# A decoder trunk with an RWKV recurrence: its small products chained in phases between dense work, and four row groups in the second channel mixer

## The chip, the cores and the metric

The kernel runs on one core of one Trainium2 chip. The metric is the device time of one execution in microseconds, as the median of several runs. A profiled execution stands beside them; its trace gives each instruction's start, duration and what it waited for.

The engines are named as in the profile: PE (TensorE, matrix products; PEld is its weight load), DVE (VectorE), ACT (ScalarE), POOL (GpSimd) and SP (SyncE, which issues the transfers).

## What is computed

The reference is one inference step of a two-layer trunk for 512 prompt tokens (one sequence) and 32 sample tokens (8 sequences of 4), with 1024 features. Every layer is a channel mixer, a token mixer and a second channel mixer, each with a normalisation ahead of it:

```python
def swiglu(x, wg, wu, wd):
    return (jax.nn.silu(x @ wg) * (x @ wu)) @ wd

for i in range(DEPTH):                                   # DEPTH = 2
    x = x + 0.5 * swiglu(rmsnorm(x, norm_ffa[i]), ffa_wg[i], ffa_wu[i], ffa_wd[i])   # D_FF = 2816
    x = x + mixer[i % 2](rmsnorm(x, norm_mix[i]))        # 0: RWKV-7, 1: mLSTM
    x = x + 0.5 * swiglu(rmsnorm(x, norm_ffb[i]), ffb_wg[i], ffb_wu[i], ffb_wd[i])
y = rmsnorm(x, norm_final)
```

The change is in layer 0, whose token mixer is a recurrence over 16 heads with a state of 64 x 64 per head. The samples start from a given state and the prompt from zero:

```python
def step(S, inp):
    r_t, d_t, k_t, v_t, kk_t, b_t = inp
    sa = jnp.einsum('bhvk,bhk->bhv', S, -kk_t)
    S = S * d_t[:, :, None, :] + sa[..., None] * b_t[:, :, None, :] + v_t[..., None] * k_t[:, :, None, :]
    return S, jnp.einsum('bhvk,bhk->bhv', S, r_t)
```

After it come a normalisation over each head, a bonus term (r k r_k) v, a gate g and the output projection wo. All states are returned too.

## The kernel before

Activations lie feature-major: eight tiles of 128 features x 544 tokens. The tokens are worked in two parts, `PARTS` = 0:256 and 256:544, the second with the samples at its end. Dense work is fp32 in two halves: `split` rounds a value to its high part (ACT, L352) and takes the difference as the low part (DVE, L353), and `mm3` makes three products of a 128 x 128 weight tile and 256 or 288 columns (L356 to L358). `weight` loads a weight block (SP), up to 1024 columns, and splits it in blocks of 512.

**The recurrence** (`rwkv`) works in chunks of 64 tokens. Two neighbouring tiles of 128 features, so four heads, go together: this is a group `m`. There are ND = 4 of them in each token part, so eight in all, of four chunks `c` each; `rwkv_slots` goes through 32 slots t = 4 m + c. What a group needs:

- `rwkv_prep`: low-rank products, decays and scaled rows (mostly DVE and ACT);
- `rwkv_quad`: masked products (L937), then the inverse of each chunk's triangular tile by doubling, five levels of two products with an ACT copy and DVE additions between them, in half precision, then one correction. Its products are 64 x 64 (name `b`); its transposes are products too (L945 for the rows `xt`);
- `rwkv_tokens`: values by token, `uv`, and the bonus;
- `rwkv_chunk`, per slot: a chain on one state: `pr` (L1059, L1061 into `pc`), a DVE copy, `pu` (L1042), two copies into `uv`, the state's product `pn` (L1048) and the output `py` (L1035, L1037), then the new state on DVE;
- `rwkv_sample`, second part only, once per feature tile: the samples' masked products, a state solve of three steps, outputs (L1127) and the new state (L1135), with POOL, ACT and DVE between;
- `rwkv_finish`, once per feature tile: centring (L1151), variance (L1155), the gate's product (L356 to L358 and L1168, into `ps`), each waiting for the one ahead of it through ACT and DVE.

**The dense work around it** are units in a list `todo`: first the projections of the second token part and the channel mixer that stands ahead of the recurrence, then (scope `rw2`) the output projection and the second channel mixer's first part, `ffn_units(*after, 0)`. That mixer goes in groups of hidden rows, `groups=(0, 8, 15, FT)` with FT = 22 tiles: the `up` units of a group (gate and up products), then eight `down` units over the group's rows, each added into x (L502). Every slot issues the group's small work and then its share of the units (`step`), counted in units.

**What sets the order.** The program's order in which the code issues work isn't the engines' order. A scheduler places the instructions of every engine when the kernel is built, from modelled times, and prefers what has high priority: small work is issued under `high_priority(OFF)`, so it goes in as soon as the model finds it ready, among the dense products. On the chip each engine then runs its list strictly in that order and waits where an operand isn't there.

Of the kernel before, what the change touches and what calls it, by code (L numbers as in the profile page):

```python
# [28 lines left out]
OFF = 20000  # L29
NMX = 19  # L30
# [218 lines left out]

class Trunk:  # L250
    def __init__(self, tc, nc, a, o, pool):
        self.tc, self.nc, self.a, self.o, self.pool = tc, nc, a, o, pool
        self.n = 0
        self.last = None
        self.hn = {}
        self.V, self.S, self.G, self.T = nc.vector, nc.scalar, nc.gpsimd, nc.tensor

# [97 lines left out]
    def mm3(self, out, wh, wl, xh, xl, start, stop):  # L355
        self.T.matmul(out, wh, xh, start=start, stop=False)  # L356
        self.T.matmul(out, wh, xl, start=False, stop=False)  # L357
        self.T.matmul(out, wl, xh, start=False, stop=stop)  # L358
# [102 lines left out]
    def ffn_units(self, name, g, i, groups=(0, 8, 15, FT)):  # L461
# [18 lines left out]
        def up(m):  # L480
            pg, pu = self.bank("pd", 2), self.bank("pd", 2)
            for ps, n in ((pg, "_g"), (pu, "_u")):
                wt = self.weight(self.a[name + n][m])
                for k in range(KT):
                    c = slice(k * P, (k + 1) * P)
                    self.mm3(ps[:, :w_], *wt(c), xs[k][0], xs[k][1], k == 0, k == KT - 1)
            s, w, e = self.t1(w_), self.t1(w_), self.t1(w_)
            V.tensor_tensor(s, pg[:, :w_], rs, op=ALU.mult)  # L488
            V.tensor_tensor(w, pu[:, :w_], rs, op=ALU.mult)
            self.sigmoid(e, s)  # L490
            G.tensor_tensor(s, s, w, op=ALU.mult)
            G.tensor_tensor(s, s, e, op=ALU.mult)
            h[m] = [self.hm(w_) for _ in range(2)]
            self.split(*h[m], s)

        def down(m, k0, k1):
            wt = self.weight(self.a[name + "_d"][m][:, k0 * P:k1 * P])
            ps = self.bank("pd", 2)
            for k in range(k0, k1):
                c = slice((k - k0) * P, (k - k0 + 1) * P)  # L500
                self.mm3(ps[:, :w_], *wt(c), h[k][0], h[k][1], k == k0, k == k1 - 1)
# [55 lines left out]
    def rwkv(self, before=None, after=None):  # L557


        with self.scope("rw", nps=1):  # L560
# [4 lines left out]
            with self.tc.tile_pool(name="spill", bufs=1, space=DRAM) as dp:  # L565
# [3 lines left out]
                self.d, self.quad, self.st = {}, {}, {}  # L569
                self.chain, self.chain_y = [self.bank("pc", 2) for _ in range(2)]  # L570
                self.nhm = {"mx": NMX, "hm": 8}
                with self.scope("rw1", nps=0):
# [7 lines left out]
                    with self.tc.high_priority(OFF):  # L580
                        self.rwkv_ahead(0)
                        self.rwkv_square(0)
# [3 lines left out]
                    with self.tc.high_priority(OFF):  # L586
                        self.rwkv_value(0)
                        self.rwkv_ahead(1)
# [4 lines left out]
                    self.rwkv_slots(10, 16)  # L593
                self.nhm = {"hm": 16}
                with self.scope("rw2", nps=0):
                    with self.tc.high_priority(OFF):
                        self.rwkv_value(ND)
                    self.rwkv_slots(16, 17)
# [100 lines left out]
    def part_dense(self, w, ps, xs, mw=P, first=True, last=True):  # L699
        for k in range(KT):  # L700
            c = slice(k * mw, (k + 1) * mw)
            self.mm3(ps, *w(c), xs[k][0], xs[k][1], first and k == 0, last and k == KT - 1)

    def rwkv_project(self, n, c, i):
# [12 lines left out]
        return [lambda: xs.extend(self.rwkv_mix(c, i))] + [lambda m=m: unit(m) for m in range(KT)]  # L717

    def rwkv_low_rank(self, i):
# [36 lines left out]
        for c, ns in ((1, (("r_w1", P, slice(0, 64), self.hwa),)), (4, (("r_a1", P, slice(64, P), self.hwa),)),  # L756
                      (5, (("r_g1a", P, slice(0, P), self.hg), ("r_g1b", P, slice(0, 96), None)))):
            us.append(lambda c=c: mix(c))
# [3 lines left out]
    def rwkv_first(self, i):  # L762

        low, k = self.rwkv_low_rank(i), self.rwkv_project("k", 2, i)
        return ([lambda: self.rwkv_norm(i)] + low[:4] + self.rwkv_project("r", 0, i) + k[:5],
# [26 lines left out]
    def rwkv_ahead(self, m):  # L792

        if m < 2 * ND:
            self.d[m] = [self.rwkv_prep(2 * (m % ND) + a, m // ND) for a in range(2)]

    def rwkv_square(self, m):
        if m < 2 * ND:
            self.quad[m] = self.rwkv_quad(self.d[m])

    def rwkv_value(self, m):
        if m < 2 * ND:
            uv = self.rp("uv", 2, [P, 1024]).rearrange("p (a c h v) -> p a c h v", a=2, c=4, h=2)
            for a in range(2):
                self.rwkv_tokens(2 * (m % ND) + a, m // ND, self.d[m][a]["v"], uv[:, a])
            self.quad[m] += (uv,)

    def rwkv_slots(self, t0, t1):

        for t in range(t0, t1):  # L810
            m, c = divmod(t, 4)
            i, j = divmod(m, ND)
            with self.tc.high_priority(OFF):
                if c == 0:
                    self.rwkv_square(m + 1)

                    if m + 1 != ND:
                        self.rwkv_value(m + 1)
# [31 lines left out]
    def rwkv_prep(self, j, i):  # L850
        nc, V, S, G, T = self.nc, self.V, self.S, self.G, self.T
# [10 lines left out]
        for e, rows in enumerate(R):  # L862
            ps = self.bank("pq", 1)[:, :w]
# [12 lines left out]
        S.activation(q, k, AF.Square, scale=self.vec("kk", j))  # L876
        ps = self.bank("pq", 1)[:, :w]
# [29 lines left out]
        return {"xc": xc, "xs": xs, "arc": arc, "ars": ars, "pc": pc, "y": k, "v": v}  # L907

    def rwkv_quad(self, ds):
# [3 lines left out]
        V, S, G, T = self.V, self.S, self.G, self.T  # L913
# [16 lines left out]
        xt = self.rp("xt", 2, [P, 1024])  # L930
# [667 lines left out]
```

## Time and profile before

| | us |
|---|---|
| median of 3 runs | 2538.42 |
| lowest and highest of them | 2537.14, 2539.9 |
| profiled execution | 2541.78 |
| its span | 2539.8 |
| PE busy in it | 2445.1 (96%) |
| DVE busy | 1587.1 (62%) |
| ACT busy | 1250.3 (49%) |
| POOL busy | 501.6 (20%) |
| mean granted clock of PE | 0.976 |

The profiled execution is 2.0 us longer than its span, and 3.4 us longer than the median. Busy time of PE holds time at a lower clock, so a high share doesn't by itself say that PE does its work at full speed: the granted clock stands beside it in the windows. Matmuls overlap one another, so the distance from one start to the next, not the duration, tells what one costs. The recurrence and the dense work around it stand from about 190 to 1236 us of the span; then follow the rest of the second channel mixer and layer 1.

### The profile page before, as it was taken

The numbers are of one execution on the slowest core, as the hardware profiler recorded it, in microseconds if no ns is written. First come the engines' busy times: TensorE is split into PE (matmuls) and PEld (weight loads), VectorE is DVE, ScalarE is ACT, GpSimd is POOL, SyncE is SP. The second block draws the span as 40 slices with busy tenths as digits, with TensorE's granted clock in tenths as the row PEclk, the third lists the DMA queues.
The fourth block names the chain that finished last, engine by engine and source line by source line (L and its number), as shares of the span: only waits on it lengthen the run. The fifth ranks groups of instructions, "written<-read, shape, count | busy, mean of one in ns | idle before, by whom it ended". The sixth has DMA issues, their size and how long they took to land.

```text
span 2539.8 us, 54086 instructions
## 1 busy us (share of the span) xinstructions
PE 2445.1 (96%) x21731; PEld 2310.1 (91%) x21731; DVE 1587.1 (62%) x3154; ACT 1250.3 (49%) x2716; POOL 501.6 (20%) x522
## 2 busy tenths in 40 slices
PE   9998999999889999999999999999999999999997
PEld 8998988888778788897899999999978899999997
DVE  6667787787887886765666544443346856444433
ACT  6555666655575564554555433332245545333322
POOL 1203333333432342322011011110000000111100
PEclk9998999999799899999999999999999999999999
DMA  6664543333233223444455522222223322222222
GB/s 215 183 197 130 166 131 120 105 96 120 90 120 103 75 93 113 129 150 146 128 167 164 153 89 90 84 85 88 83 87 112 101 73 92 86 92 90 88 84 73
DMA packets 102218, 291.62 MB, mean 115 GB/s; under 512 B 12568, under 2 KB 28344, under 8 KB 101968
## 3 DMA queue, kind: packets, MB, share of 16 engines
q1 hardware_dynamic: 101968, 288.18, 36.9%
q8 instruction: 170, 2.79, 0.4%
q14 instruction: 80, 0.66, 0.1%
HBM read 278.76 MB, written 9.38 MB: 113 GB/s over the span
## 4 chain that ended last, share of the span: by engine, by line
PE 84%; DVE 9%; issue 2%; ACT 2%; DMA 1%; POOL 1%; SPq 0%; DVEq 0%; ACTq 0%; POOLq 0%
PE ps L356 17%; PE ps L358 17%; PE ps L357 17%; PE pd L356 7%; PE pd L357 7%; PE pd L358 7%; DVE wl L353 2%; DVE m L693 1%; PE ps L1254 1%; PE ps L1256 1%; PE ps L1255 1%; PE b L937 1%; PE ps L1135 1%; DVE mx L695 1%; PE pc L1059 1%
## 5 line engine op out<-in xcount | busy, mean ns | idle before, releaser
L353 DVE TENSOR_TENSOR wl<-wr,wh 128x512 fp32r<-128x512 f32 (+2 forms) x1025 | 723.2, 708 | 479.6 <-ACT wh L352 452.8
L352 ACT CAST wh<-wr 128x512 fp32r<-128x512 f32 (+2 forms) x1025 | 621.8, 609 | 676.6 <-PE ps L357 430.8
L356 PE MATMUL ps<-a,wh 128*128 128x288 f32 (+1 forms) x2384 | 698.0, 293 | 13.5 <-ACT a L404 5.0
L358 PE MATMUL ps<-a,wl 128*128 128x288 f32 (+1 forms) x2384 | 692.6, 291 | 0.0
L357 PE MATMUL ps<-a,wh 128*128 128x288 f32 (+1 forms) x2384 | 686.6, 288 | 0.3
L356 PEld LDWEIGHTS ps<-a,wh 128*128 128x128 f32 x2384 | 452.8, 190 | 16.9 <-DVE raw L1350 5.4
L357 PEld LDWEIGHTS ps<-a,wh 128*128 128x128 f32 x2384 | 452.6, 190 | 1.5 <-DVE a L405 0.8
L358 PEld LDWEIGHTS ps<-a,wl 128*128 128x128 f32 x2384 | 450.0, 189 | 0.5 <-DVE wl L353 0.2
L428 POOL TENSOR_TENSOR t<-t,t 128x256 f32<-128x256 f32 (+1 forms) x132 | 141.7, 1073 | 846.7 <-ACT wh L352 410.1
L356 PE MATMUL ps<-h,wh 128*128 128x288 f32 (+1 forms) x1056 | 303.9, 288 | 0.0
L357 PE MATMUL ps<-h,wh 128*128 128x288 f32 (+1 forms) x1056 | 303.4, 287 | 0.0
L358 PE MATMUL ps<-h,wl 128*128 128x288 f32 (+1 forms) x1056 | 303.2, 287 | 0.0
L356 PE MATMUL pd<-rk,wh 128*128 128x288 f32 (+1 forms) x656 | 199.0, 304 | 6.8 <-DVE t L488 2.9
L358 PEld LDWEIGHTS ps<-h,wl 128*128 128x128 f32 x1056 | 198.9, 188 | 0.0
L357 PEld LDWEIGHTS ps<-h,wh 128*128 128x128 f32 x1056 | 198.9, 188 | 0.0
L357 PE MATMUL pd<-rk,wh 128*128 128x288 f32 (+1 forms) x656 | 198.6, 303 | 0.2 <-DVE gm L679 0.2
L356 PEld LDWEIGHTS ps<-h,wh 128*128 128x128 f32 x1056 | 198.6, 188 | 0.0
L358 PE MATMUL pd<-rk,wl 128*128 128x288 f32 (+1 forms) x656 | 197.2, 301 | 0.0
L352 ACT CAST h<-t 128x256 fp32r<-128x256 f32 (+1 forms) x132 | 55.3, 419 | 198.9 <-POOL t L428 198.9
L357 PE MATMUL pd<-mx,wh 128*128 128x256 f32 (+1 forms) x448 | 135.3, 303 | 9.4 <-DVE mx L695 6.6
L356 PE MATMUL pd<-mx,wh 128*128 128x256 f32 (+1 forms) x448 | 133.8, 302 | 4.3 <-ACT rk L716 1.9
L356 PEld LDWEIGHTS pd<-rk,wh 128*128 128x128 f32 x656 | 128.0, 195 | 10.5 <-ACT mx L694 2.9
(460 smaller groups left out, 4548.4 us busy)
## 6 DMA issues: line engine op xcount, KB each, us to landing
wr<-in_f0a_u_dram SPq DMA_DIRECT2D x44, 512.0 KB, 3.6
wr<-in_f0b_g_dram SPq DMA_DIRECT2D x44, 512.0 KB, 3.6
wr<-in_f0b_u_dram SPq DMA_DIRECT2D x44, 512.0 KB, 3.5
wr<-in_f0a_g_dram SPq DMA_DIRECT2D x43, 512.0 KB, 3.6
wr<-in_f0b_d_dram SPq DMA_DIRECT2D x24, 512.0 KB, 3.6
wr<-in_f1a_g_dram SPq DMA_DIRECT2D x22, 512.0 KB, 4.6
wr<-in_f1a_u_dram SPq DMA_DIRECT2D x22, 512.0 KB, 3.5
wr<-in_f1b_g_dram SPq DMA_DIRECT2D x22, 512.0 KB, 3.5
```

The costliest lines, as they stand in the source:

```text
L352: self.S.copy(dst_h, src)
L353: self.V.tensor_tensor(dst_l, src, dst_h, op=ALU.subtract)
L356: self.T.matmul(out, wh, xh, start=start, stop=False)
L357: self.T.matmul(out, wh, xl, start=False, stop=False)
L358: self.T.matmul(out, wl, xh, start=False, stop=stop)
L428: self.G.tensor_tensor(s, s, w, op=ALU.mult)
L693: V.scalar_tensor_tensor(m, d, self.vec("mu", c * 8 + k), xn, op0=ALU.mult, op1=ALU.add)
L695: (self.G if k % 2 else V).tensor_tensor(l, m, h.bitcast(F32), op=ALU.subtract)
L937: T.matmul(pg[:, (1 - h) * 512 + i * P:(1 - h) * 512 + (i + 1) * P], flat(xc[R[h], i]), flat(arc[R[h], i]), start=True, stop=True)
L1059: T.matmul(py[R[h], out(a)], uv[:, a, c, h, :], gm[:, a, c, 1 - h, 64:128], start=True, stop=st is None)
L1135: T.matmul(pn[R[h], :], xt[H, h * 64:(h + 1) * 64], um, start=True, stop=True)
L1254: T.matmul(pss[q][:n, :], xs[k][0][:, ts], wt(cs)[0], start=k == 0, stop=False)
```

## The change

Six things change, all in layer 0's recurrence and what is interleaved with it:

1. The functions `rwkv_prep`, `rwkv_quad`, `rwkv_tokens`, `rwkv_chunk`, `rwkv_sample` and `rwkv_finish` become generators, which stop ahead of each of their products at a place "s", "pq" or "ps". Every slot has SPS = 4 steps; in each, a phase advances the running generators by one product group, a share of dense work follows, a second phase (places "pq" and "ps") and another share.
2. Within a phase, products go through a wrapper `Plain`: the first is put at ordinary priority, and each next one is made to follow the one before it on PE (`t.after`).
3. Dense work is counted in products (`Unit` with a cost for each part), not in units, and an `up` unit can be parted between its gate and its up half.
4. The samples of a group are two pairs of feature tiles' worth of work in six phases (masked products; right-hand side; three solve steps; outputs and state), with more buffers, and the transposes in one bank. The finishes are phases as well, spread over the next slots.
5. In the quad the transposes into `tt` share a bank with the residual, and the row transposes `xt` move into a function of their own, `rwkv_rows`. The state's update in the chunk is issued behind the output's products.
6. The second channel mixer's prompt part has four row groups, (0, 6, 11, 17, 22), so 32 instead of 24 `down` units; `hm` has 12 instead of 16 buffers, and slot 16 belongs to the first scope.

```diff
+SPS = 4
+    def put(self, f, a, k):
+        t = self.t
+        if not t.group:
+            r = f(*a, **k)
+        elif t.order is None:
+            with t.tc.high_priority(-t.off):
+                r = f(*a, **k)
+            t.order = r
+        else:
+            r = f(*a, **k)
+            t.after(r, t.order)
+            t.order = r
+        return r
...
-    def ffn_units(self, name, g, i, groups=(0, 8, 15, FT)):
+    def ffn_units(self, name, g, i, groups=(0, 6, 11, 17, FT)):
...
+            return Unit((24, lambda: half("_g")), (24, second))
...
-            us += [lambda m=m: up(m) for m in range(k0, k1)]
-            us += [lambda m=m, k0=k0, k1=k1: down(m, k0, k1) for m in range(KT)]
+            us += [up(m) for m in range(k0, k1)]
+            us += [Unit((3 * (k1 - k0), lambda m=m, k0=k0, k1=k1: down(m, k0, k1))) for m in range(KT)]
...
-                    self.rwkv_slots(10, 16)
-                self.nhm = {"hm": 16}
+                    self.rwkv_slots(10, 17)
+                self.nhm = {"hm": 12}
...
+    def rwkv_phase(self, places):
+
+        with self.tc.high_priority(OFF):
+            self.off = OFF
+            self.group, self.order = True, None
+            seen = set()
+            for name in list(self.gens):
+                place = self.gens[name][1]
+                if place in places and (place == "s" or place not in seen):
+                    seen.add(place)
+                    if place != "s":
+                        self.order = None
+                    self.advance(name)
+            self.off, self.group = 0, False
...
+        def dense():
+            nonlocal done, k
+            k += 1
+            while todo and done + todo[0][0] / 2 <= total * k / n:
+                c, f = todo.pop(0)
+                done += c
+                f()
...
-                if c == 2:
-                    self.rwkv_ahead(m + 2)
-                if i and c in (0, 1):
-                    self.rwkv_sample(2 * j + c, self.d[m][c])
-                self.rwkv_chunk(m, c)
+                if i and c == (m == ND):
+                    self.begin("sample", self.rwkv_samples(m))
+                if c == 2:
+                    self.begin("ahead", self.rwkv_ahead(m + 2))
+                self.begin("chunk", self.rwkv_chunk(m, c))
+                self.off = 0
+            for q in range(SPS):
+                self.rwkv_phase(("s",))
+                dense()
+                self.rwkv_phase(("pq", "ps"))
+                dense()
+            with self.tc.high_priority(OFF):
+                self.off = OFF
+                self.drain("chunk")
                 if c == 3:
-                    for a in range(2):
-                        self.rwkv_finish(2 * j + a, i, m)
-            self.step(-(-len(self.todo) // (t1 - t)))
+                    self.drain("finish", "sample")
+                    self.begin("finish", self.rwkv_finishes(m))
...
-        pt = pb()
-        each(lambda r, a, b: T.matmul(pt[r, a], ti[r, a], id16[r], start=True, stop=True))
-        S.copy(tt, pt[:, :W])
+        yield "s"
         pr = pb()
+        each(lambda r, a, b: T.matmul(pr[r, b], ti[r, a], id16[r], start=True, stop=True))
```

How the built order moves is seen at two places on PE. The first is a step of the chunk chain in the first half of the recurrence (438 to 443 us of the trace). `pc` is the chain's bank, `b` and `pq` are the quad's banks, `pd` a dense product's; a row with x4 is four in a row. Before:

```order
L1059 MATMUL pc_2716<-gm_4565,uv_6059 64x64
L358 MATMUL pd_5987<-mx_5454,wl_5991 128x256
L356 MATMUL pd_5987<-mx_5460,wh_5990 128x256
L1048 MATMUL pc_2715<-uv_6059,xt_4566 64x64 x4
L1059 MATMUL pc_2716<-gm_4565,uv_6059 64x64
L1061 MATMUL pc_2716<-a_934_4487,sm_6636 64x64
L937 MATMUL b_6187<-a_1230_6138 128x128
L1061 MATMUL pc_2716<-a_934_4487,sm_6636 64x64
L1059 MATMUL pc_2716<-gm_4565,uv_6059 64x64
L937 MATMUL b_6187<-a_1230_6138 128x128 x7
L945 MATMUL pq_6204<-c_c_all_79,a_1230_6138 128x128 x4
```

After, at the same step of the chain:

```order
L282 MATMUL pc_2715<-uv_6058,xt_4566 64x64 x4
L282 MATMUL pc_2716<-gm_4565,uv_6058 64x64 x2
L282 MATMUL pc_2716<-a_934_4487,sm_6372 64x64 x2
L282 MATMUL pc_2716<-gm_4565,uv_6058 64x64 x2
L282 MATMUL pc_2716<-a_942_4529,sm_6372 64x64 x2
L398 MATMUL pd_6749<-rk_522_2735,wh_6752 128x288
```

The chain's products stood one by one between dense products and the quad's; now those of one phase stand in one row (all of them have the wrapper's line, L282), and dense work follows.

The second place is the end of the recurrence on PE (1195 to 1215 us of the trace): the last sample's output and state, then the two last finishes (`ps` is their bank; `rk` or `a` with the constants `c_c_rw` is a centring or a variance product). Before:

```order
L1127 MATMUL ps_17328<-sa_17270,sa_17287 64x32 x2
L357 MATMUL pd_17885<-rk_2985_16647,wh_17892 128x288
L358 MATMUL pd_17885<-rk_2984_16646,wl_17893 128x288
L1135 MATMUL ps_17333<-um_17334,sa_17282 64x512
L1135 MATMUL ps_17333<-um_17337,sa_17282 64x512
L1151 MATMUL ps_17697<-rk_1987_10581,c_c_rw_2701 128x288
L1155 MATMUL ps_17701<-a_516_2727,c_c_rw_2701 128x288
L356 MATMUL ps_17712<-a_519_2731,a_520_2732 128x288
L357 MATMUL ps_17712<-a_519_2731,a_520_2732 128x288
L358 MATMUL ps_17712<-a_519_2731,a_520_2732 128x288
L1168 MATMUL ps_17712<-a_520_2732 128x288
L1151 MATMUL ps_17723<-rk_2007_10704,c_c_rw_2701 128x288
```

After, the centring of the first of these finishes, and 27 dense products further the variance (transposes and products of the wrapper have L276 or L282):

```order
L399 MATMUL pd_17665<-hm_17612,wh_17661 128x256
L400 MATMUL pd_17665<-hm_17611,wl_17662 128x256
L276 MATMUL ps_17868<-rk_1981_10503,c_c_rw_2701 128x288
L398 MATMUL pd_17698<-hm_17147,wh_17690 128x256
L399 MATMUL pd_17698<-hm_17148,wh_17690 128x256
```

```order
L399 MATMUL pd_17725<-hm_17494,wh_17717 128x256
L400 MATMUL pd_17725<-hm_17493,wl_17718 128x256
L276 MATMUL ps_17872<-a_516_2727,c_c_rw_2701 128x288
L398 MATMUL pd_17725<-hm_17611,wh_17721 128x256
L399 MATMUL pd_17725<-hm_17612,wh_17721 128x256
```

The links of the finishes stood next to each other at the end; now `down` products of the second channel mixer stand between them.

## Rows read from the trace of the kernel before

**Rows 1.** The page: busy time by engine; PE's granted clock in 40 slices, tenths.

```profile
PE 2445.1 (96%) x21731; PEld 2310.1 (91%) x21731; DVE 1587.1 (62%) x3154; ACT 1250.3 (49%) x2716; POOL 501.6 (20%) x522
...
PEclk9998999999799899999999999999999999999999
```

**Rows 2.** Windows: stretch, length, busy PE PEld DVE ACT POOL, clock, DMA share, GB/s.

```profile
353.00:636.00 283.00, 275.55 (x3453) 248.39 (x3451) 223.81 (x439) 171.88 (x397) 101.47 (x94) 0.99 0.37 112
636.00:669.00 33.00, 23.86 (x221) 19.61 (x213) 28.68 (x58) 17.21 (x54) 20.80 (x41) 0.64 0.19 56
669.00:745.00 76.00, 70.93 (x504) 66.41 (x503) 60.55 (x122) 52.22 (x125) 15.36 (x16) 0.96 0.40 125
745.00:780.00 35.00, 24.79 (x202) 20.43 (x201) 34.51 (x67) 23.68 (x58) 17.86 (x16) 0.80 0.22 69
780.00:1195.00 415.00, 404.84 (x4731) 352.71 (x4730) 295.69 (x626) 226.17 (x527) 129.75 (x133) 0.97 0.39 120
1195.00:1236.00 41.00, 32.52 (x183) 26.92 (x182) 22.55 (x46) 20.19 (x42) 1.03 (x1) 0.83 0.28 86
1236.00:2540.00 1304.00, 1278.04 (x9870) 1249.72 (x9868) 668.05 (x1327) 525.93 (x1081) 134.25 (x142) 0.99 0.33 101
```

**Rows 3.** Timeline of PE: start, duration, line, out<-in, tiles, count, [wait <-releaser].

```profile
438.33 0.28 PE L356 MATMUL pd<-mx,wh 128*128 128x256 f32 x1
438.44 0.28 PE L357 MATMUL pd<-mx,wh 128*128 128x256 f32 x1
438.65 0.33 PE L1059 MATMUL pc<-gm,uv 128*64 128x64 f32 x2
438.91 0.39 PE L358 MATMUL pd<-mx,wl 128*128 128x256 f32 x1
439.14 0.28 PE L356 MATMUL pd<-mx,wh 128*128 128x256 f32 x1
...
440.51 0.32 PE L1061 MATMUL pc<-a,sm 64*64 64x64 f32 x2
440.77 0.33 PE L1059 MATMUL pc<-gm,uv 128*64 128x64 f32 x2
...
443.82 0.28 PE L1037 MATMUL pc<-sm,a 64*64 64x64 f32 x4
443.93 0.28 PE L1035 MATMUL pc<-uv,gm 64*64 64x64 f32 x4
...
1194.94 0.29 PE L357 MATMUL pd<-rk,wh 128*128 128x288 f32 x1
1195.07 0.30 PE L358 MATMUL pd<-rk,wl 128*128 128x288 f32 x1
```

**Rows 4.** Timeline of PE in the first starved stretch, columns as in rows 3.

```profile
647.25 0.69 PE L1042 MATMUL pc<-sm,tf 64*64 64x64 f32 x8 [3.22 <-DVE sm L1039]
...
657.57 0.44 PE L357 MATMUL pd<-mx,wh 128*128 128x288 f32 x1
657.80 0.44 PE L358 MATMUL pd<-mx,wl 128*128 128x288 f32 x1
```

**Rows 5.** Timeline of PE at the end of the recurrence, columns as in rows 3.

```profile
1198.74 1.07 PE L1135 MATMUL ps<-um,sa 64*64 64x512 f32 x2 [1.24 <-POOL um L1133]
...
1207.26 1.33 PE L1151 MATMUL ps<-rk,c_c_rw 128*128 128x288 f32 x2 [1.80 <-DVE rk L1169]
...
1214.72 0.81 PE L356 MATMUL pd<-rk,wh 128*128 128x288 f32 x2 [2.34 <-ACT rk L352]
```

**Rows 6.** Windows of 100 us, columns as in rows 2.

```profile
400.00:500.00 100.00, 99.00 (x1156) 88.57 (x1155) 79.53 (x162) 66.24 (x155) 30.54 (x30) 1.00 0.35 106
600.00:700.00 100.00, 88.11 (x986) 77.75 (x985) 76.71 (x159) 60.19 (x158) 37.90 (x57) 0.85 0.32 98
```

**Rows 7.** Groups of DVE instructions: line, out<-in, shapes, count, busy, mean ns, idle before.

```profile
L353 DVE TENSOR_TENSOR wl<-wr,wh 128x512 fp32r<-128x512 f32 x961 | 691.3, 722 | 455.5 <-ACT wh L352 428.8 <-PE pd L358 2.7 <-ACT uv L1011 1.1
L353 DVE TENSOR_TENSOR wl<-wr,wh 128x256 fp32r<-128x256 f32 x32 | 13.6, 425 | 18.6 <-ACT wh L352 18.6
```

More of the change, by code (lines that the diff above doesn't have):

```diff
@@ L247, in __getitem__, with __init__, __call__, matmul @@
         return self.d[k + self.by]
+class Unit:
+    def __init__(self, *parts):
+        self.parts = parts
+    def __call__(self):
+        for _, f in self.parts:
+            f()
+class Plain:
+    def __init__(self, t, engine):
+        self.t, self.engine = t, engine
+    def matmul(self, *a, **k):
+        return self.put(self.engine.matmul, a, k)
+    def transpose(self, *a, **k):
+        return self.put(self.engine.transpose, a, k)
+    def put(self, f, a, k):
[11 more added lines that the diff above has]
+        return r
 class Trunk:
@@ L256, in __init__ @@
         self.V, self.S, self.G, self.T = nc.vector, nc.scalar, nc.gpsimd, nc.tensor
+        self.off, self.PT = 0, Plain(self, nc.tensor)
+        self.order, self.group = None, False
+        self.gens = {}
     def tile(self, tag, bufs, shape, dt=F32):
@@ L480, in up, with half, second @@
         def up(m):
[L481 to L494, printed above, removed]
+            ps = []
+            def half(n):
+                ps.append(self.bank("pd", 2)[:, :w_])
+                self.part_dense(self.weight(self.a[name + n][m]), ps[-1], xs)
+            def second():
+                half("_u")
+                s, w, e = self.t1(w_), self.t1(w_), self.t1(w_)
+                V.tensor_tensor(s, ps[0], rs, op=ALU.mult)
+                V.tensor_tensor(w, ps[1], rs, op=ALU.mult)
+                self.sigmoid(e, s)
+                G.tensor_tensor(s, s, w, op=ALU.mult)
+                G.tensor_tensor(s, s, e, op=ALU.mult)
+                h[m] = [self.hm(w_) for _ in range(2)]
+                self.split(*h[m], s)
+            return Unit((24, lambda: half("_g")), (24, second))
         def down(m, k0, k1):
@@ L498, in down @@
             ps = self.bank("pd", 2)
[L499 to L501 removed]
+            self.part_dense(wt, ps[:, :w_], [h[k] for k in range(k0, k1)])
             V.scalar_tensor_tensor(self.x[m][:, hs], ps[:, :w_], 0.5, self.x[m][:, hs], op0=ALU.mult, op1=ALU.add)
@@ L568, in rwkv @@
                 self.v = [[t[:, hs] for t in self.x] for hs in PARTS]
-                self.d, self.quad, self.st = {}, {}, {}
+                self.d, self.quad, self.st, self.xt, self.uv = [{} for _ in range(5)]
                 self.chain, self.chain_y = [self.bank("pc", 2) for _ in range(2)]
@@ L697, in rwkv_mix, with part_dense @@
         return r
-    def part_dense(self, w, ps, xs, mw=P, first=True, last=True):
-        for k in range(KT):
+    def part_dense(self, w, ps, xs, mw=P):
+        for k in range(len(xs)):
             c = slice(k * mw, (k + 1) * mw)
-            self.mm3(ps, *w(c), xs[k][0], xs[k][1], first and k == 0, last and k == KT - 1)
+            self.mm3(ps, *w(c), xs[k][0], xs[k][1], k == 0, k == len(xs) - 1)
     def rwkv_project(self, n, c, i):
@@ L716, in unit @@
             self.S.copy(t, ps)
-        return [lambda: xs.extend(self.rwkv_mix(c, i))] + [lambda m=m: unit(m) for m in range(KT)]
+        return [Unit((0, lambda: xs.extend(self.rwkv_mix(c, i))))] + [lambda m=m: unit(m) for m in range(KT)]
     def rwkv_low_rank(self, i):
@@ L794, in rwkv_ahead @@
         if m < 2 * ND:
-            self.d[m] = [self.rwkv_prep(2 * (m % ND) + a, m // ND) for a in range(2)]
+            self.d[m] = []
+            for a in range(2):
+                yield from self.rwkv_prep(2 * (m % ND) + a, m // ND, self.d[m])
     def rwkv_square(self, m):
         if m < 2 * ND:
-            self.quad[m] = self.rwkv_quad(self.d[m])
+            yield from self.rwkv_quad(m, self.d[m])
     def rwkv_value(self, m):
@@ L993, in rwkv_quad, with rwkv_rows @@
         V.tensor_tensor(tf, tt, pf[:, :W], op=ALU.add)
-        return gm, tf, xt
+        self.quad[m] = gm, tf, self.xt[m]
+    def rwkv_rows(self, m):
+        self.xt[m] = xt = self.rp("xt", 2, [P, 1024])
+        for a, d in enumerate(self.d[m]):
+            yield "pq"
+            px = self.bank("pq", 1)
+            for i in range(4):
+                self.PT.transpose(px[:, i * P:(i + 1) * P], d["xc"][:, i].rearrange("p x t -> p (x t)"), self.ident)
+            self.S.copy(xt[:, a * 512:(a + 1) * 512], px)
     def wide_bank(self):
@@ L1124, in rwkv_sample @@
                 V.tensor_tensor(uv[Q[0], 1, :], rhs[Q[0]], pu[Q[0], :64], op=ALU.add)
-        py = self.ps()
+        ums = []
+        for h in range(2):
+            um = self.local("um", 2, [64, 512])
+            G.tensor_tensor(um.rearrange("p (b v) -> p b v", b=NB), uv[H, h, :].unsqueeze(1).to_broadcast([64, NB, 64]),
+                            self.seqm[H].unsqueeze(2).to_broadcast([64, NB, 64]), op=ALU.mult)
+            ums.append(um)
+        yield "s"
+        py = self.bank("pq", 1)
         for h in range(2):
```

177 lines of the change are left out of this document (114 added, 63 removed).

## The prediction

> **What bounds the kernel now.** I read the page first, then windows of busy time, then stretches of the timeline. The page has TensorE (PE) busy 96% of the span and VectorE (DVE) 62%, so PE sets the time; but PE's granted clock has a digit of 7 in the slice from 635 to 698 us and an 8 in the one from 825 to 889 [rows 1]. The built orders of the two kernels name the stretch that the change can touch: PE's products are the same 20,228 in both, in the same order up to 353 us and from about 1236 us on. So only 883 us, the recurrence with the dense work around it, are in play.
>
> The windows cut these 883 us at the places where PE falls behind [rows 2]. In each, idle time is the length less PE's busy time: 7.5 us in 353 to 636, 9.1 in 636 to 669, 5.1 in 669 to 745, 10.2 in 745 to 780, 10.2 in 780 to 1195, 8.5 in 1195 to 1236, together 50.5 us. To that comes time at the lower of the two clock levels (1.2 instead of 2.4 GHz; a granted clock of 0.64 is a mean of the two). A dense step is 0.13 us at full clock and 0.23 at half [rows 3, 4], so a granted clock c costs about busy time x (1-c) x 0.92: 2.5, 7.9, 2.6, 4.6, 11.2 and 5.1 us, together 34. **Some 84 us of the stretch are not full-clock work**, and a reordering has that to win, plus what each change of tile shape costs. From 1236 us on PE has 1278 of 1304 us at 0.99 and the change leaves it alone.
>
> What the losses wait for differs. In 636 to 669 and 745 to 780, DVE is busy 28.7 of 33 and 34.5 of 35 us: the tile solves, the preparation of the next pair and the weight splits meet there, and PE waits up to 3.2 us for one link [rows 4]. In 1195 to 1236 no engine is near its limit; there PE does the last pair's sample and two finishes one link after the other, and each waits: 1.24, 1.80, 2.34 us among others [rows 5].
>
> **The change part by part.** First, **the tail**. Before, the last sample and the finishes come after nearly all dense work is given out, so their links stand back to back. After, the finishes are phases, and in the built order 27, 18, 30, 28 and 24 dense products stand between their links, some 3 us each at 0.12 us [rows 3], above the longest wait there (2.34 us) [rows 5]. That covers the 8.5 us of idle time and so the cause of the half clock. I take 12 of the 13.6 us; the bounds are 8 (idle alone) and 13.6. What hides the links is dense work that four row groups leave for the end: without it the 12 go.
>
> Second, **the two starved stretches**, 17.0 and 14.8 us lost (idle plus clock). The "quad" (the doubling of the tile inverse), the preparation and the next values no longer come in one block at a slot's start but in phases spread over the slot, with dense work between. PE's wait can go, DVE's work can't: 347.6 us of it stand in the 427 us of 353 to 780, which is 81%. Taking all losses there (49.5 us) would put DVE at 92%. In a stretch that PE has under control DVE was at 80% (79.5 of 100 us) [rows 6], and in the worst at 98.6%. I take 20 of the 31.8 us here and, third, 5 of the 17.7 us of **353 to 636 and 669 to 745**, which sets DVE at 347.6 of 402, 86%. Bounds: 0 (DVE has no more to give) and 41 (DVE at 90%) for the two together. Some help comes with this: in the built order the links of the chunk chain that have under 1 us of other PE work ahead of them fall from 6 to 1 of 95. Some hindrance too: of the quad's links 22 instead of 12 have under 2 us of cover.
>
> Fourth, **780 to 1195**: 21.4 us lost with DVE at 71% and POOL at 31% [rows 2], so nothing but the order stands against a return. Before, a sample pair stood as one block of thirteen links with one dependence after another; after, as six phases a quarter of a slot apart. I take 12, a bit over half, as the clock's loss (11.2) is spread thin; bounds 0 and 21.
>
> Fifth, **changes of tile shape**. Within a phase small products are chained, so that dense work doesn't split them, and the quad's transposes share a bank with its residual. In the built orders PE goes from dense work into small products 196 times instead of 248 in the stretch, and changes its tile shape 105 times fewer. The rows price it: into a visit 0.21 us instead of a step of 0.12, out of it 0.23 instead of 0.12, a change inside a run 0.26 instead of 0.11 [rows 3]: 0.09, 0.11 and 0.15 us. I take their mean, 0.12, since most but not all of the 105 are ends of visits: 105 x 0.12 = 13 us, bounds 9.5 and 16. The Trainium skill's page "TensorEngine Tiling (Array Packing)", section Key Properties, says that a switch of tiling mode drains TensorE; if that meant the whole 0.28 us that a row gives one dense product, the term would be 29 instead of 13, and the rows, with 0.09 to 0.15 us, show less than that.
>
> Sixth, **what is added**. Four row groups instead of three in the second channel mixer's prompt part (32 instead of 24 down units): 8 more additions into x at 0.43 us on DVE, the price of 256 columns [rows 7], 16 more pairs of splits of 128 columns and 16 of 256 against 16 fewer of 384 (a 256 takes 0.43, a 512 0.72, a 384 about the 0.57 between) [rows 7], 8 more weight loads on SP. That is about 3.4 + 16 x 0.43 + less than 7 - 16 x 0.57 = under 9 us of DVE in a stretch where it is at 71%, hidden behind PE; I charge 2 us, bounds 0 and 9. The DMA engines are busy 0.39 of the time there [rows 2]. The first slot of the second half now stands ahead of the change of scope at 780, and smaller hm buffers (12 for 16) free sooner; both are within the second and fourth terms.
>
> The sum: 12 + 20 + 5 + 12 + 13 - 2 = **60 us** off the profiled execution's 2541.8, which is 2482. The median of the runs shown is 3.4 us under that execution, so **2478**.
>
> **The rivals.** *DVE takes over* (chance 0.20): the phases only move PE's waits, and 353 to 780 is done when DVE's work is done. For it: 34.5 of 35 us [rows 2], and that 691 of DVE's 1587 us are full weight splits (961 of 0.72 us) [rows 1, 7], whose number doesn't fall. Against it: 86% is well under that. Then the second and third terms give nothing, nor half of the shape term: 12 + 12 + 6 - 2 = 28, so 2510.
>
> *Chained phases make PE wait in order* (0.10, slower): PE takes its program strictly in order. Where a phase's first product waits for DVE, ScalarE or POOL, everything behind it waits too: its own chain and the dense work after it. Before, single small products slipped in between dense ones; now a phase is placed whole, at a place counted in dense products and not in time. For it: 3.22 us of wait at one such link [rows 4], and 10 more quad links with little cover. Against it: there are more dense products between phases than before in the chunk chain. It decides from 60/196 = 0.31 us of new waiting a visit on; at 0.6 us it costs 118 us, which gives 2538 + 58 = 2596.
>
> *Longer small runs cost clock* (0.05). In 400 to 500 us PE held a granted clock of 1.00 with many small products in 1156, in 600 to 700 it had 0.85 with 88 us busy [rows 6]: the clock fell where PE idled, not where it did small products. But if longer runs of 64-row products (19.4 on average instead of 15.3) let it fall, one us at half clock in every second visit, as in 98 visits, would be 98 x 0.46 = 45 us back: 2523. The Trainium skill's "TensorE: Matmul & The Clock Gate" says, in its part on the transpose mode, that transposes don't count as PE-busy in the same way for the clock; by that rule packing them together would bring this about. The rows at 1.00 speak against it.
>
> *It doesn't do what it says* (0.05): the waits are those of the dependences, and come back at other places; shape changes hide under the weight loads. That is 2538.
>
> **How the numbers follow.** Forecast 2478, 0.60; DVE 2510, 0.20; in-order waits 2596, 0.10; clock 2523, 0.05; no effect 2538, 0.05. The range must leave out no more than 0.2. Down: the highest values of the terms are 13.6 + 41 + 21 + 16 - 0 = 92, or 2446. Up: it takes in DVE and the clock, 2528 with some 5 us of the added work. Faster by over 0.2% (5 us, about what a measurement of this kernel can tell from no change): forecast, DVE and clock, 0.85. Within it 0.05. Slower 0.10.
>
> **What would show each step.** Tail: in the 41 us before the dense end (1236 us, earlier in the changed kernel) no wait over 1 us and clock near 1.0. Starved stretches: the clock at the places of the quad of pairs two and three above 0.9 and PE idle under 5 us each; if DVE shows 95% and more there with PE waiting for it, the DVE rival is right. 780 to 1195: mean clock 0.99. Shape: the sum of waitless steps of small products falls by some 13 us. In-order waits would show as rows of PE with an idle time before the first product of a phase, many of 0.5 us and more. The prediction is wrong if the changed kernel's PE idles above 50 us in the stretch, or if the part behind it differs from 1304 us by more than 5.

## The result: 34 us faster, with its gain in other places than forecast

The changed kernel takes 2504.62 us (median of 4, 2500.67 to 2506.71), the kernel before 2538.8: a ratio of 0.9864, 95% interval 0.9847 to 0.9881, or 34 us. The forecast was 2478 (2446 to 2528). The profiled execution of the changed kernel is its fastest, 2500.67 us with a span of 2498.4. The two profiled executions are 41 us apart, where the medians are 34 apart.

The page after, lines as in [rows 1]:

```profile
PE 2407.4 (96%) x21731; PEld 2286.8 (92%) x21731; DVE 1588.1 (64%) x3178; ACT 1253.0 (50%) x2733; POOL 504.8 (20%) x522
...
PEclk9999999998899899999999999999999999999998
```

PE's busy time is down by 38 us with the same instructions. The clock still has its digits of 8. Windows of the changed kernel, columns as in [rows 2], cut where its losses stand; the same last 9870 PE instructions begin at 1199 instead of 1236 us:

```profile
353.00:600.00 247.00, 237.23 (x2829) 219.01 (x2828) 196.09 (x371) 153.91 (x342) 89.82 (x84) 0.99 0.41 123
600.00:660.00 60.00, 42.73 (x461) 33.94 (x461) 56.54 (x108) 33.55 (x95) 35.88 (x54) 0.72 0.22 69
660.00:725.00 65.00, 64.23 (x647) 60.04 (x643) 50.31 (x98) 42.83 (x99) 11.62 (x13) 1.00 0.42 132
725.00:755.00 30.00, 23.68 (x231) 20.02 (x229) 28.99 (x58) 19.92 (x50) 15.18 (x14) 0.89 0.16 48
755.00:800.00 45.00, 43.13 (x598) 38.03 (x598) 29.66 (x66) 25.53 (x61) 5.78 (x6) 1.00 0.38 124
800.00:830.00 30.00, 23.69 (x319) 18.37 (x319) 22.25 (x51) 15.82 (x40) 10.40 (x10) 0.89 0.04 11
830.00:880.00 50.00, 48.30 (x615) 41.32 (x614) 39.12 (x98) 30.73 (x77) 8.91 (x10) 0.90 0.37 107
880.00:1158.00 278.00, 273.43 (x3265) 243.17 (x3264) 211.20 (x466) 162.09 (x390) 109.96 (x112) 1.00 0.43 130
1158.00:1199.00 41.00, 40.28 (x309) 38.99 (x308) 31.92 (x69) 27.22 (x59) 0.00 (x0) 1.00 0.56 167
1199.00:2498.40 1299.40, 1276.56 (x9870) 1248.47 (x9868) 666.71 (x1327) 526.83 (x1082) 135.29 (x142) 0.99 0.33 101
```

With the prediction's own formula (length less PE's busy time; busy time x (1-clock) x 0.92), the losses are:

| stretch, before / after | before: idle + clock | after: idle + clock |
|---|---|---|
| 353 to 780 / 353 to 755 | 31.9 + 17.6 = 49.5 | 34.1 + 15.6 = 49.7 |
| 780 to 1195 / 755 to 1158 | 10.2 + 11.2 = 21.4 | 14.5 + 6.8 = 21.3 |
| last 41 us / last 41 us | 8.5 + 5.1 = 13.6 | 0.7 + 0 = 0.7 |
| the rest: PE's work at full clock | 798.6 | 774.3 |

The stretch became 37 us shorter: 13 in the tail, 24 in PE's full-clock work, nothing net in the 830 us between. (The other 4 us of the two profiled executions' 41 lie outside the stretch, where the change does nothing; runs of one kernel differ by as much.) "Nothing net" hides a shift: the first starved place lost 17.0 us in 33 and now loses 28.3 in 60, the second 14.8 and now 8.7, and the rest of 353 to 780 lost 17.7 and now 12.7.

In the second row of the table, too, the losses stand together. In the kernel before 11.6 of the 21.4 us lie in one piece of 60 us, with DVE busy 51.6 of them (columns as in [rows 2]):

```profile
830.00:890.00 60.00, 53.89 (x703) 43.78 (x701) 51.58 (x113) 32.09 (x79) 23.74 (x21) 0.89 0.24 79
```

The longest waits of PE in the changed kernel's starved stretch, 600 to 665 us (for whom, us in total, times, longest):

```profile
PE b L279 <- DVE ti L1095: 2.9, 2, 2.4
PE pd L399 <- DVE mx L737: 2.2, 3, 1.0
PE pd L429 <- DVE rms L416: 2.1, 1, 2.1
PE ps L279 <- DVE rk L1317: 2.0, 1, 2.0
```

and DVE's costliest groups in 600 to 660 us, columns as in [rows 7]:

```profile
L735 DVE SCALAR_TENSOR_TENSOR m<-hm,c_vecs,x 128x288 f32<-128x288 f32 x24 | 17.0, 729 | 1.0 <-POOL mx L737 0.8
L737 DVE TENSOR_TENSOR mx<-m,mx 128x288 fp32r<-128x288 f32 x11 | 7.4, 668 | 0.1
```

DVE is busy 56.5 of these 60 us, with hardly any idle time ahead of its instructions. Its main load there is not the quad (L1095: 6 instructions, 3.8 us) but the normalisation of the second token part and three token-shift mixings in a row (`rwkv_norm`, `rwkv_mix`; 17.0 + 7.4 us for the mixings), between which the program has only the 48 products of two low-rank units. My reading is that the quad's and the finishes' small steps stand behind the mixing in DVE's list, and that PE waits for them; the runs without the mixing below test it.

### The profile page after: what moved, and what is told of

Read it like the earlier page. It is cut to its first block, busy times and chain, and to the rows that moved or that the text cites. A ratio compares the mean times of both kernels' runs of the same rounds, so it can differ in the third digit from the quotient of the medians.

```text
span 2498.4 us, 54146 instructions
## 1 busy us (share of the span) xinstructions
PE 2407.4 (96%) x21731; PEld 2286.8 (92%) x21731; DVE 1588.1 (64%) x3178; ACT 1253.0 (50%) x2733; POOL 504.8 (20%) x522
## 4 chain that ended last, share of the span: by engine, by line
PE 60%; DVE 2%; ACT 1%; issue 1%; DMA 1%; POOL 0%; SPq 0%; DVEq 0%; ACTq 0%; POOLq 0%
PE ps L398 15%; PE ps L400 15%; PE ps L399 15%; PE pd L398 3%; PE pd L399 2%; PE pd L400 2%; PE ps L282 1%; PE pc L282 1%; PE ps L1402 1%; PE ps L1404 1%; PE ps L1403 1%; DMA d<-dc 0%; DVE wl L394 0%; PE ps L279 0%; PE b L282 0%
## 5 line engine op out<-in xcount | busy, mean ns | idle before, releaser
L394 DVE TENSOR_TENSOR wl<-wr,wh 128x512 fp32r<-128x512 f32 (+2 forms) x1041 | 731.4, 706 | 471.8 <-ACT wh L393 446.3
L398 PE MATMUL pd<-rk,wh 128*128 128x288 f32 (+1 forms) x656 | 194.4, 297 | 3.2 <-DVE t L532 2.4
L399 PE MATMUL pd<-rk,wh 128*128 128x288 f32 (+1 forms) x656 | 193.8, 296 | 2.0 <-DVE rk L447 1.9
L468 DVE TENSOR_TENSOR t<-ps,rms 128x256 f32<-128x256 f32 (+1 forms) x132 | 58.1, 440 | 123.0 <-PE ps L400 123.0
```

Of the source, the lines that this page charges most:

```text
L394: self.V.tensor_tensor(dst_l, src, dst_h, op=ALU.subtract)
L468: self.V.tensor_tensor(w, pu[:, :w_], rs[i], op=ALU.mult)
```

## The experiments

My theory after the result: the tail is gained by spreading, the full-clock work by fewer visits to small products, and the middle stays because DVE has it. The rival: the prediction's sizes (0.12 us a change of shape; phases that take waits away everywhere), with something else giving back part. All ratios are to the kernel before, run beside. Differences to the changed kernel are between medians of different comparisons; the kernel before had medians of 2538.8 to 2540.2 us in these, so a difference of a few us says little.

**What a visit costs, by itself.** Extra 64 x 64 products ahead of layer 1's 176 accumulations of gate and up products, where PE does dense work alone; `{n}` is 1 or 4.

```diff
                 for ps, wt in ((pg, wg), (pu, wu)):
+                    for _ in range({n} if name in ("f1a", "f1b") else 0):
+                        self.T.matmul(ps[:64, :64], self.ident[:64, :64], self.ident[:64, :64], start=True, stop=True)
```

> The changed kernel with one extra 64 x 64 product (64 columns, full fp32) ahead of each of the 176 accumulations of gate and up products in layer 1's two channel mixers, into the bank that the accumulation then overwrites. There PE has 1277 of 1299 us busy and no small products, so each one is a visit of its own: 352 more changes of tile shape. By the three rows of the prediction (0.09 us in, 0.11 us out, about 0.1 us for the product) a visit costs 0.3 us: +53 us, 2558. By what the result suggests (24 us for 105 fewer changes, 0.23 us each) it costs 0.46 + 0.1 us: +99 us, 2603.

Measured: 2584.29 us (1.0172, 1.0157 to 1.0187), 79.7 over the changed kernel.

> As the kernel with one extra product at each of the 176 places, but four in a row: the same 352 changes of tile shape, 528 products more. The difference of the two prices one small product that stands behind its like, 0.08 to 0.13 us: 42 to 69 us above the kernel with one. What is left of that kernel's cost, less one such product, is the price of the visit by itself.

Measured: 2643.39 us (1.0410, 1.0395 to 1.0426), 59.1 over the kernel with one: 0.112 us a product behind its like. (Each of these products is two instructions in the trace, hence x2 below.) A visit with one product is 79.7/176 = 0.45 us, so the visit by itself costs **0.34 us**: neither of the two values. PE's timeline with one product (columns as in [rows 3]):

```profile
1600.31 0.28 PE L400 MATMUL ps<-a,wl 128*128 128x256 f32 x1
1600.52 0.33 PE L462 MATMUL ps<-c_c_all 64*64 64x64 f32 x2
1600.77 0.40 PE L398 MATMUL ps<-a,wh 128*128 128x288 f32 x1
1601.01 0.29 PE L399 MATMUL ps<-a,wh 128*128 128x288 f32 x1
```

Three steps are longer, not two: into the visit 0.21 us instead of 0.12, the small product 0.25 instead of about 0.12, out of it 0.24 instead of 0.13. That is 0.09 + 0.13 + 0.11 = 0.33 us a visit. 52 visits fewer are 17 to 18 us, of the 24 found, if the visits that were saved cost what these do; they hold products of other shapes too.

**Without the chaining**, all else kept:

```diff
-            self.group, self.order = True, None
+            self.group, self.order = False, None
```

> The changed kernel without the chaining: the phases, the counting of dense work and the four row groups stay, but each small product has high priority of its own, as before the change. The built order has 710 changes of tile shape instead of 675. If the gain comes from changes of shape at 0.23 us: +8 us, 2513. At the prediction's 0.12 us: +4 us, 2509. If chained rows make PE wait in order (the slower rival), this kernel is faster than the changed one by 5 us or more. If the chaining carries the whole gain by another way, it is back at 2535.

Measured: 2509.64 us (0.9886, 0.9870 to 0.9903), 5.0 over the changed kernel. The order has 22 more visits, which at 0.34 us are 7.5. By windows of 20 us over the stretch, idle time and clock loss together are what they are in the changed kernel (73 and 72 us), and the full-clock work is 8 us longer, which fits. The 5.0 us by themselves are not clear of the noise, as the two intervals overlap; but the rival that chaining makes PE wait had this kernel 5 us or more faster, and it isn't.

**The finishes in a block**, at the end of each group's last slot:

```diff
                     self.begin("finish", self.rwkv_finishes(m))
+                    self.drain("finish")
```

> The changed kernel with the two finishes of a group given out whole at the end of the group's last slot, as before the change, instead of one link in a phase. If the tail's gain (13.6 us) comes from the finishes being spread, it is lost: +12 to +14 us, 2517 to 2519, and the last 40 us of the recurrence show waits over 1 us again. If the dense work that is left for the end hides them in any order: within 3 us of 2505. The waits of 2.05, 1.74 and 3.83 us that finishes have in 600 to 755 us may go or stay; DVE is at 90% there, so I expect them to stay with other names.

Measured: 2523.13 us (0.9934, 0.9920 to 0.9949), 18.5 over: more than the tail. Windows of this kernel, the last 43 us of its stretch and the piece of the middle that got worse most:

```profile
1180.00:1223.00 43.00, 39.13 (x276) 37.55 (x275) 30.97 (x64) 27.39 (x57) 0.00 (x0) 0.96 0.49 149
...
1013.00:1033.00 20.00, 14.62 (x180) 12.40 (x182) 14.42 (x26) 7.61 (x21) 8.90 (x9) 0.66 0.21 57
```

The tail gives back only 3.9 us of idle time and 1.4 of clock. Every group ends with finishes, and they cost at other ends too. In 1013 to 1033 this kernel loses 10 us, with PE waiting 2.6 us in one piece for a finish's product with the gate (`PE ps L282 <- DVE rk L1318`), where the changed kernel loses 4.6 in all of 880 to 1158. It isn't so everywhere: 593 to 673 loses 25 us, 4 less than in the changed kernel. Over the whole stretch, in windows of 20 us, idle time is 55 instead of 49 us and the clock's loss 33 instead of 23. The spread finishes do help the middle, then; it is a net of nothing there, not an absence of effects.

**The sample pairs in a block**:

```diff
-                if i and c == (m == ND):
-                    self.begin("sample", self.rwkv_samples(m))
+                if i and c - (m == ND) in (0, 1):
+                    a = c - (m == ND)
+                    self.all_of(self.rwkv_sample(2 * j + a, self.d[m][a]))
```

> The changed kernel with each sample pair given out whole at the start of a slot, as before the change (its products in the new, shorter form), and the phases for the rest. The built order has 724 changes of tile shape instead of 675. At 0.17 us each, as the inserted products price them, that is +8 us: 2513. If the six phases also take waits away (the prediction's fourth term, 12 us in the second half of the recurrence), it comes to 2525. If the phases of the samples bring nothing: 2505.

Measured: 2519.49 us (0.9923, 0.9906 to 0.9941), 14.9 over. By windows of 20 us its idle time is 51 us and its clock's loss 23, as in the changed kernel (49 and 23); its full-clock work is 12 us longer. So nearly all of what the sample phases bring is PE's own steps, and not waits. The 24 visits fewer at 0.34 us are 8 of the 12; the other 4 are open.

**Four row groups alone**, in the kernel before:

```diff
-    def ffn_units(self, name, g, i, groups=(0, 8, 15, FT)):
+    def ffn_units(self, name, g, i, groups=(0, 6, 11, 17, FT)):
```

> The kernel before with one part of the change alone: four row groups (0, 6, 11, 17, 22) in the second channel mixer's prompt part. It adds 8 down units. If the four groups by themselves bring the cover of the tail, -10 to -14 us, 2525 to 2529. If the spread finishes do (my view now): within 4 us of 2539, with 0 to 2 us more for the added work.

Measured: 2538.15 us (0.9995, 0.9984 to 1.0007): nothing. The tail is as before, too (idle 6.8 and clock 6.6 us in its last 41). The converse, three groups in the changed kernel, wasn't tried.

**Without five of the second part's six mixings**, in either kernel; the other projections of that part take the first mixing's tiles, so what is computed from there on is other data. With DVE's part of these mixings go their casts on ACT and half of their subtractions, which are on POOL:

```diff
+        self.mixed = []
...
+        if i and self.mixed:
+            return self.mixed
         r = []
+        if i:
+            self.mixed = r
```

> The kernel before without five of the six token-shift mixings of the second token part: all projections of that part take the first mixing's tiles. That leaves out 40 of DVE's instructions of 0.73 us and 20 of 0.67 us (some 42 us), with their share of ACT and POOL, and no product. If DVE's mixing starves PE in 636 to 669 and 745 to 780 us: -20 to -30 us, 2509 to 2519, with the clock above 0.9 there. If PE waits there for the order of the quad's and the chain's links alone: under -8 us.

Measured: 2520.26 us (0.9925, 0.9907 to 0.9942), 19.3 under the kernel before.

> The changed kernel without the same five mixings. The new phases lose 28 us in 600 to 660 and 9 us in 725 to 755 us. If DVE's mixing is the cause: -25 to -35 us, 2470 to 2480. If the phases' own waits are: under -10 us. Against the kernel before without the mixings this tells whether DVE hid what the phases bring: the gap of 34 us stays if they bring nothing in the middle, and grows to 55 to 60 us if the prediction's second and third terms (25 us) were only hidden by DVE.

Measured: 2484.43 us (0.9786, 0.9763 to 0.9808), 20.2 under the changed kernel. Windows of the kernel before without the mixings, at its starved places:

```profile
636.00:669.00 33.00, 25.12 (x282) 21.46 (x281) 24.09 (x51) 17.14 (x53) 16.84 (x37) 0.74 0.28 86
745.00:780.00 35.00, 32.45 (x379) 29.72 (x378) 32.51 (x71) 25.32 (x64) 9.24 (x9) 1.00 0.40 126
```

The place at 745 is filled: PE 32.5 of 35 us at full clock, against 24.8 at 0.80 [rows 2]. The one at 636 is relieved a little. The mixing thus costs about 20 us in either order (DVE's share is my reading; these runs don't part it from ACT's and POOL's), and the gap between the kernels stays (36 us): **the phases' gain in the middle was not hidden by the mixing; it isn't there.** That part of my theory, which made DVE's mixing the whole cause, falls: without it 40 us of idle time (by windows of 20 us) are left in both kernels. At the first starved place of the changed kernel (593 to 673) some 21 of 29 us of loss are left; what they wait for, no run settles.

**The mixings in another place.** First the receptance projection ahead of the low-rank units, in the second part only:

```diff
-        return ([Unit((0, lambda: self.rwkv_norm(i)))] + low[:4] + self.rwkv_project("r", 0, i) + k[:5],
+        return ([Unit((0, lambda: self.rwkv_norm(i)))] + (self.rwkv_project("r", 0, i) + low[:4] if i else low[:4] + self.rwkv_project("r", 0, i)) + k[:5],
```

> The changed kernel with the second token part's units in another order: the receptance projection (one mixing, 192 products) ahead of the two low-rank ones (one mixing and 24 products each), instead of behind them. Everything is still computed. In the changed kernel three mixings (8.5 us of DVE each) stand behind the normalisation with 48 products between them, which is 6 us of PE. If this bunch of DVE work is what starves PE in 600 to 660 us, one of three gaps is covered by 25 us of dense work: -5 to -12 us, 2493 to 2500. If DVE's total in the stretch is what counts, not its place: within 3 us of 2505.

Measured: 2497.47 us (0.9831, 0.9815 to 0.9848), 7.2 under the changed kernel and the fastest complete kernel here (the two intervals touch at 0.985; they come from different comparisons with the kernel before). By windows of 20 us its idle time is 46 us and its clock's loss 19, against 49 and 23, which is the same 7. A window of it:

```profile
600.00:660.00 60.00, 46.77 (x516) 40.75 (x516) 49.53 (x96) 32.96 (x91) 28.14 (x46) 0.86 0.31 93
```

DVE has 49.5 instead of 56.5 us there and PE 46.8 at 0.86 instead of 42.7 at 0.72; 725 to 755 is worse (PE 21.7 us at 0.77 instead of 23.7 at 0.89). Two further orders of the second part's units:

```diff
+        if i:
+            return ([Unit((0, lambda: self.rwkv_norm(i)))] + self.rwkv_project("r", 0, i) + low[:2] + k + low[2:4],
+                    self.rwkv_project("v", 3, i) + low[4:])
```

> The changed kernel with the second token part's units in an order in which no more than two mixings stand next to each other: normalisation, receptance (192 products), first low-rank unit, key (192), second low-rank unit, value (192), gate's low-rank units. Everything is computed. Putting receptance first gave 7 us. If a bunch of mixings is what starves PE, taking apart the bunches of three and two that were left gives some more: 2488 to 2494. If only the first bunch behind the normalisation mattered: 2497 as with receptance first.

```diff
+        if i:
+            return ([Unit((0, lambda: self.rwkv_norm(i)))] + low[:2] + self.rwkv_project("r", 0, i) + low[2:4] + k[:5],
+                    k[5:] + self.rwkv_project("v", 3, i) + low[4:])
```

> As the kernel with the mixings taken apart, but with the first low-rank unit straight behind the normalisation and the second behind the receptance, so that two mixings stand behind the normalisation instead of one, and the gate's behind the value's as there. If the bunch at the normalisation is what matters: slower than that kernel by 3 to 6 us, 2494 to 2500. If the count of bunches is: the same within 3 us.

Measured: 2509.84 (0.9887, 0.9867 to 0.9906) and 2505.95 us (0.9881, 0.9856 to 0.9905): no gain over the changed kernel, whose interval overlaps both of theirs. These two say less than I wrote: the value's projection writes over x, from which the gate's mixing reads, so the gate is computed from other data and its mixing has to wait for the values. They don't decide whether the bunch matters.

Last, receptance first and a part of the mixing moved from DVE to POOL:

```diff
-            (self.G if k % 2 else V).tensor_tensor(l, m, h.bitcast(F32), op=ALU.subtract)
+            (self.G if k % (4 if i else 2) else V).tensor_tensor(l, m, h.bitcast(F32), op=ALU.subtract)
```

> The changed kernel with the receptance projection ahead of the low-rank ones (7 us faster by itself), and with six instead of four of every eight subtractions of the second part's mixing on POOL: 12 times 0.56 us go from DVE to POOL, where one takes 1.0 us. Leaving out 37 us of DVE's mixing gave 20 us, 0.54 us for each; by that rate the 6.8 us moved give 3 to 4 us: 2493 to 2495. If POOL, which has 36 of 60 us busy around the mixing, takes over as the engine that is waited for: 2498 to 2503.

Measured: 2504.88 us (0.9859, 0.9843 to 0.9876): the 7 us are gone. PE's waits for the mixing's subtraction on POOL, 590 to 760 us, with receptance first alone and then in this kernel:

```profile
PE pd L399 <- POOL mx L737: 2.8, 3, 1.2
...
PE pd L399 <- POOL mx L737: 4.1, 5, 1.2
```

The waits for POOL grew by 1.3 us while those for the same step on DVE fell by 1.0 (1.9 to 0.9), so the move gains nothing at its own place. By its time this is the second case of the expectation, and a little past it; but these waits don't make 7 us. By windows of 20 us the largest loss that came back is in 853 to 873 (7.3 instead of 0.9 us), behind all mixings, and why is open.

## Why the prediction held, and where its steps failed

The range held and the sign was right; the size was 34 where 60 was forecast, nearer to the case in which DVE takes over (2510). That the time came within the range is partly luck: three terms of 37 us together brought nothing, and PE's full-clock work fell by 24 us where 13 were forecast. Step by step:

- *The tail* (12 us): right, 12.9 by the windows, at a clock of 1.00. Its reason was half right. Four row groups alone bring nothing, so their dense work by itself doesn't do it; whether it is needed beside the phases, no run shows. (The 18 products between two of the links are 2.2 us, not above the longest wait; it made no difference.) With the finishes in a block most of the tail stays covered, and with the samples in a block the finishes still are. It takes the phases of both to bring the old tail back, which I infer from the two runs; both undone together wasn't run.
- *The starved stretches and the rest of 353 to 780* (20 + 5 us): failed; 49.5 us of loss before and 49.7 after, where 25 of them were to go. The step that failed is the one from "DVE has 81% over 427 us" to "PE's wait can go". DVE's work isn't spread as that mean has it: it comes in bunches whose place is set by the list of dense units. There a normalisation or a mixing counts as one unit before and as no product after, and in neither by its time on DVE; DVE's scalings for the first three mixings start within 25 us before (L693, 644 to 669) and 32 us after (L735, 625 to 657). The runs without the mixings show about 20 us of the 50 for this; the rest stays open. I blamed the solves and the preparation; the groups of DVE in that stretch, a view of before that I had and read too coarsely, name the mixing (L693: 12.1 of DVE's 28.7 us in 636 to 669).
- *780 to 1195* (12 us): failed as a whole, 21.4 before and 21.3 after. The step that failed is again a mean: DVE at 71% over 415 us, and losses taken as spread thin, where over half of them stood in 830 to 890 with DVE at 86%. In 880 to 1158 the changed kernel loses 4.6 us; but 800 to 880 has 14.8. There the last finishes of the first token part stand on PE link by link, the output projection that needs them begins at 817 us and runs on from 828, and hardly a weight is loaded (11 GB/s). The prediction gave that boundary no term.
- *Changes of tile shape* (13 us, bounds 9.5 and 16): mis-sized. I priced each change at the mean of three rows, 0.12 us, and 105 changes. A visit, that is two changes, pays for the step in, the first small product and the step out: 0.33 us, so 52 visits give 17 to 18 us. The price stood in [rows 3]: from 438.44 to 439.14 us one visit takes three steps of 0.70 us together, which without it would be some 0.35. The sample phases and the chaining, undone, show the same kind of price. The full-clock work fell by 24; for the last 6 to 7 us of it I have no experiment.
- *The added work* (2 us): not seen; DVE's busy time rose by 1 us in all.
- *The clock's price* (0.92 of busy time x (1-clock)): the steps named, 0.13 and 0.23 us, give 0.87. That takes 2 us off the 34 and changes nothing else.
- *Of the rivals*: in-order waits show no sign (without the chaining it isn't faster), nor does a clock lost to long small runs (0.976 before, 0.981 after). DVE's takeover gave the right time for a part of the right reason.
- *Of the signs*: the tail's came. Those of the starved stretches didn't: the clock is 0.72 in 600 to 660 us instead of above 0.9, with 17 us idle instead of under 5, and 755 to 1158 has a clock of 0.98 instead of 0.99. DVE is at 94% there and at 97% in 725 to 755, which is about the sign of its takeover. The two that were to show the prediction wrong stayed just short: 49.3 us idle in the stretch (limit 50), and a part behind it 4.6 us shorter (limit 5).

Undone one at a time, finishes, sample phases and chaining cost 18.5, 14.9 and 5.0 us, 38 together against a gain of 34. If they add, these three account for the gain about once; that they do isn't shown, as no run undoes all three. Two parts of the change were never undone by themselves: dense work counted in products, and the quad's shared bank with its separate row transposes.

## What to carry to other kernels

Price a break in a stream of products by its whole visit (the step in, the first small product, the step out), not by an average of its steps, and count visits in the built order: here that gives 17 to 18 of the 24 us by which the full-clock work fell. Where an engine starves another, list its costliest instructions in that very stretch before saying which of them move: work that a list of products counts as nothing still takes another engine's time. And spread short chains of links through the program: the finishes in a block cost 18.5 us here, some 5 of them at the last end.

## What I had not expected of the hardware

The first small product of a run (64 x 64, two instructions) takes 0.25 us and one behind its like 0.11, so most of a lone small product's price is its being alone: 0.45 us with everything, four times that of one more in a row. A dense product of 256 columns takes 0.12.
